# Second layer of a feed-forward block on one Trainium2 core: the rows of the third step move to the first two row places, and the weights of the first product are issued behind the rows of the step ahead

## The chip, the cores and the metric

The kernel runs on one core of a Trainium2 chip. The metric is the time of the slowest core in device microseconds, here of the only one; a kernel's time is the median of its runs. Before the change that is 1913.62 us over three runs, from 1910.7 to 1918.03 us.

## The reference, cut to what matters

One decoder layer over 2048 positions of width 1024: a normed input projection, a pooling mixer and a causal stick-breaking attention, an output projection, then a feed-forward block of inner width 4096 and a last norm. The change lies in the second matrix of the feed-forward block, `w_down`:

```python
        hn2 = rmsnorm(h, norm2_g)
        up = jnp.einsum('bsd,df->bsf', hn2, w_up)
        act = jnp.square(jax.nn.relu(up))
        h = h + jnp.einsum('bsf,fd->bsd', act, w_down)
    return rmsnorm(h, final_g)
```

All of it is float32.

## The kernel before

**Number format.** A float32 operand is split into a high half of the matmul's own type and the rest (`split`: ScalarE copies the high half, line 146, and VectorE subtracts it from the operand, line 147). A product of two float32 tiles is then three matmuls: high by high, high by low, low by high. So no matmul of a step can start before ScalarE's half of the split, and the second one needs VectorE's half too.

**The two layers.** Both feed-forward matrices are multiplied by a seven-product scheme on 2x2 blocks (Strassen's, in Winograd's form). `up` forms the first layer and writes the row sums that the second layer wants to DRAM (`sd`, and `sdi` for the products that are split a second time), all through the SyncE queue SP at lines 884 and 1013. `down` is the second layer. Its products come in the order P1, P6, P7, P4, P5, P2, P3. P1 and P6 have eight steps each, P7 to P2 are split once more into small steps (line 1274), and P3 ends the kernel.

**A step of P1.** `make(g)` prepares step g: it loads one block of weights (`blk`, line 1162, tile `wr`, 512 KB), loads two tiles of rows, one for each pair of token tiles (`ar<-sd`, line 1222, 512 KB each), and splits the weights into `wd` and the rows into two `ad`. The step itself (line 1451) is 48 matmuls, 24 on the first row tile and then 24 on the second. `make_ahead` keeps up to six row tiles and three weight blocks ahead of the matmuls. The first step is made in advance under high priority, the second behind the tile `A22` of the last column of `up`, the rest behind its tile `S3`.

**Places.** Row tiles `ar` lie in two pools: `rs` has two places (`early`), `rs2` three (`late_`). A running number `turns["ar"]` picks the pool in `row`: below 2 it is `rs`, from there on the places are gone through in a ring of five, two of `rs` and three of `rs2`. The number starts at -2, and each step of P1 takes two, so the rows of the first and of the second step lie in `rs`, those of the third in `rs2`. Split rows `ad` have a ring of five as well, split weights `wd` three places (`DA + 1`).

**What sets the order.** Each engine runs its instructions in one fixed order, which a scheduler makes when the kernel is built: it plays through a timeline by rules of its own, and `tc.issue_after(x)` keeps an instruction behind x in it. In P1 the rows of a step are held behind `last[0]`, the row load before them; the weights are not held. All loads and stores named here are issued by SP, in its fixed order. Each of them also waits for one of eight completion counters (`DMAHW0` to `DMAHW7`, used in turn), that is for the transfer eight places ahead of it; a wait named `DVE` is one for VectorE.

Of the kernel before, what the change touches and what calls it, by code (L numbers as in the profile page):

```python
# [46 lines left out]
def hymba_block(ctx: ExitStack, tc: tile.TileContext, xT, gains, w_in, pool_w, w_out, w_up, w_down, out):  # L47
# [95 lines left out]
    def split(dst, src):  # L143

        hi, lo = dst
        nc.scalar.activation(hi, src, AF.Copy)  # L146
        return nc.vector.tensor_tensor(lo, src, hi.bitcast(F32), ALU.subtract)  # L147
# [970 lines left out]
    def down(pools):  # L1118
# [9 lines left out]
            else:  # L1128
                steps += [(n, i, kk, (0, 1)) for kk in range(8)]
        steps += [("P3", S4, kk, (q,)) for q in range(2) for kk in range(8)]  # L1130
        made, turns, extra = {}, {"ar": -2, "ad": 0}, []

        def row(shape, kind, tag, **kw):
            early, late_ = {"ar": rs, "ad": s8}[tag]
            n = turns[tag]
            turns[tag] += 1
            return (early if n < 2 or n % 5 < 2 else late_).tile(shape, kind, tag=tag, name=tag, **kw)
# [11 lines left out]
        def inner_weights(i, kk, t):  # L1149

            if kk < 4:
                tops[i] = t
                return
            b, k = {(x, y): half(w, y) for x, w in enumerate((tops.pop(i), t)) for y in range(2)}, kk - 4
            for to, x, y, p in (((0, 0), (0, 1), (0, 0), "P5"), ((0, 1), (1, 1), (0, 1), "P7"),
                                ((1, 1), (1, 1), (0, 0), "P6"), ((1, 0), (1, 0), (1, 1), "P4")):
                nc.vector.tensor_tensor(b[to], b[x], b[y], ALU.subtract)
                nc.sync.dma_start(wi[i][p][k // 2][:, 2 * (k % 2):2 * (k % 2) + 2], b[to])

        def blk(i, kk, where=None):  # L1160
            t = (where or rt).tile([P, 4, 256], F32, tag="wr", name="wr")
            nc.sync.dma_start(t, w_down[i, kk] if isinstance(i, int) else td[int(i[1]) - 1][kk])
            return t

        def minus(a, b):
            nc.vector.tensor_tensor(b, a, b, ALU.subtract)
            return b

        def more_weights(n, kk, w):

            if n == "P1" and kk % 4 < 2:
                inner_weights(A12, kk, blk(2, kk))
            elif n == "P6":
                minus(blk(2, kk, rtx), w)
                nc.sync.dma_start(half(td[1][kk], 0), half(w, 0))
                if kk >= 4:
                    nc.sync.dma_start(half(td[1][kk], 1), half(w, 1))
                inner_weights(A22, kk, w)

        def make_inner(n, p, kk):  # L1180

            i, kp = SPLIT[n], kk // 2
            if kk % 2 == 0:
                if p in wi[i]:
                    w = rt.tile([P, 4, 256], F32, tag="wr", name="wq")
                    nc.sync.dma_start(w, wi[i][p][kp])
                else:
                    w = quarter(source[n], kp, *{"P1": (0, 0), "P2": (1, 0), "P3": (1, 1)}[p])
                t = made["inner"] = t8.tile([P, 2, 4, 256], F32R, tag="wd", name="wd", align_bytes=256)
            r = row([P, 2, T], F32, "ar")  # L1190
            nc.sync.dma_start(r, {"P1": sd[0][i][kk], "P2": sd[0][i][kk + 4], "P4": sd[1][i][kk + 4]}[p]
                              if p in ("P1", "P2", "P4") else sdi[i][("P5", "P6", "P7", "P3").index(p)][kk])
            if kk % 2 == 0:
                split((t[:, 0], t[:, 1]), w)
            a = row([P, 2, 2, T], F32R, "ad", align_bytes=256)
            split((a[:, 0], a[:, 1]), r)
            return made["inner"], a

        def make(g):
            n, i, kk, qs_ = steps[g]  # L1200
            if qs_ is None:
                at = {("P7", "P5"): 3, ("P5", "P5"): 2}.get((n, i))
                if at is not None and kk == 0:
                    extra[:] = [blk(2, at), blk(2, at + 4)]
                elif at is not None and kk == 3:
                    for k in range(2):
                        inner_weights(A12, at + 4 * k, extra.pop(0))
                made[g] = make_inner(n, i, kk)
                return
            if n != "P3":  # L1210
                kk = TURN[kk]
            b11, b12, b21, b22 = range(4)
            if n == "P1":
                w = blk(b11, kk)
            elif n == "P6":
                w = minus(blk(b22, kk), blk("t1", kk))
            else:
                w = blk(b22, kk)
            rows = {q: row([P, 2, T], F32, "ar") for q in qs_}
            for q in qs_:  # L1220
                with tc.issue_after(last[0].ins) if n == "P1" and last[0] else nullcontext():
                    last[0] = nc.sync.dma_start(rows[q], sd[q][i][kk])
            t = t8.tile([P, 2, 4, 256], F32R, tag="wd", name="wd", align_bytes=256)
            split((t[:, 0], t[:, 1]), w)
            left_ = {}
            for q in qs_:
                left_[q] = row([P, 2, 2, T], F32R, "ad", align_bytes=256)
                last[1] = split((left_[q][:, 0], left_[q][:, 1]), rows[q])
            while late and n != "P1":
                late.pop(0)()  # L1230
            late.append(lambda: more_weights(n, kk, w))
            made[g] = t, left_
# [179 lines left out]
        free, held, ahead, late, last = 4, [], [0, 0, 0], [], [None, None]  # L1412
# [10 lines left out]
        def make_ahead(limit=len(steps)):  # L1423

            while ahead[0] < limit and (ahead[1] + lefts(ahead[0]) <= 6 and ahead[2] + stationary(ahead[0]) <= 3):
                make(ahead[0])
                ahead[1] += lefts(ahead[0])
                ahead[2] += stationary(ahead[0])
                ahead[0] += 1
# [109 lines left out]
    def ffn():  # L1539
        catch_up(len(later))  # L1540
        front_scope.close()
        for _ in layer.pop():
            pass
        left_scope.close()
        with ExitStack() as scope:
            spool = lambda name, bufs, **kw: scope.enter_context(tc.tile_pool(name=name, bufs=bufs, reuse_waits="tile", **kw))

            rlp, pupa = spool("rlp", 2), spool("pupa", 2)
            spool("even", 1).tile([P, 2 * P // 4], F32, name="even")
            rs = spool("rs", 2), spool("rs2", 3)  # L1550
            rt, t8 = spool("rt", 6), spool("t8", DA + 1)
            s8 = spool("s8", 2), spool("s82", 2 * DA - 1)
            tmp2, pup, rtx = spool("tmp2", 2), spool("pup", 6), spool("rtx", 1)
            down([t8, s8, rs, rt, pupa, pup, rtx, rlp, tmp2, spool("psb", 1, space=PS)])
# [88 lines left out]
```

## Time and profile before

| | |
|---|---|
| median of three runs | 1913.62 us |
| the profiled execution's own time | 1912.54 us |
| its span on the core | 1910.7 us |
| TensorE matmul busy | 1882.5 us, 99% |
| VectorE, ScalarE, GpSimd busy | 77%, 54%, 9% |
| data moved | 535.91 MB, 280 GB/s over the span |
| TensorE idle ahead of line 1451 | 7.4 us, once |
| second layer: first matmul of line 1451, last one | 1311.1 us, 1884.0 us |

The profile names a group of instructions by line, engine, operation and tiles, as `pb<-ad,wd`, and puts the idle time of an engine down to what ended it. `PEclk` is the granted TensorE clock as a share of full speed, the DMA share that of the 16 DMA engines that were busy. Times inside the execution are counted from the start of its span.

### The profile page before, as it was taken

How to read it: one execution, taken by the hardware profiler on the slowest of the kernel's cores; microseconds unless marked ns; L12 is line 12 of the kernel's file. 1: busy time of each engine (PE TensorE's matmuls, PEld its weight loads, DVE VectorE, ACT ScalarE, POOL GpSimd, SP SyncE). 2: the span in 40 equal slices, each digit the busy share in tenths (PEclk: the TensorE clock that was granted, in tenths of full speed). 3: DMA queues.
4: the chain of work that ended last, by engine and by line, in shares of the span. 5: the costliest groups of instructions: out<-in, count | busy, mean ns of one | idle time of the engine just before them, and what ended most of it. 6: DMA issues, size and time to landing. Idle time of an engine off the chain costs nothing.

```text
span 1910.7 us, 26756 instructions
## 1 busy us (share of the span) xinstructions
PE 1882.5 (99%) x8947; PEld 1571.0 (82%) x8947; DVE 1480.3 (77%) x2216; ACT 1025.6 (54%) x1616; POOL 180.5 (9%) x399
## 2 busy tenths in 40 slices
PE   9999999999999999999999999998999999999997
PEld 7888888888888888888888888887788888888886
DVE  6887799667866886778789988886556677889774
ACT  6565566555554465554567455554332665656543
POOL 0211123101211030000000000000010010020120
PEclk9999999999999999999999999999999999999999
DMA  7686686888787777887898988889898999999852
GB/s 225 207 271 187 209 283 217 259 303 266 278 328 290 279 245 253 289 311 273 316 342 324 317 302 279 292 294 346 311 314 300 321 318 309 328 303 346 285 209 91
DMA packets 222164, 535.91 MB, mean 280 GB/s; under 512 B 26048, under 2 KB 32192, under 8 KB 218176
## 3 DMA queue, kind: packets, MB, share of 16 engines
q1 hardware_dynamic: 217264, 525.46, 79.4%
q0 software_dynamic: 4608, 8.39, 2.5%
q8 instruction: 72, 1.18, 0.2%
q14 instruction: 76, 0.62, 0.1%
q10 hardware_dynamic: 144, 0.26, 0.0%
HBM read 349.46 MB, written 184.55 MB: 279 GB/s over the span
## 4 chain that ended last, share of the span: by engine, by line
PE 43%; DMA 7%; DVE 5%; issue 1%; ACT 1%; POOL 0%; SPq 0%; DVEq 0%; ACTq 0%
PE pb L1274 16%; PE pb L1451 12%; PE pY L1102 8%; PE pZ L1102 4%; PE pX L1102 2%; DMA t<-in_w_down_dram 2%; DMA sd<-s 1%; DVE hw L147 1%; DMA hn<-hs 1%; PE pb L1391 1%; DMA td<-t 1%; DMA wi_P<-t 1%; DMA sd<-a 1%; DMA ar<-sd 0%; ACT a L1019 0%
## 5 line engine op out<-in xcount | busy, mean ns | idle before, releaser
L1102 PE MATMUL pY<-sa,hw 128*128 128x512 f32 x1536 | 366.2, 389 | 1.6 <-ACT u L1025 1.2
L1102 PEld LDWEIGHTS pY<-sa,hw 128*128 128x128 f32 x1536 | 288.1, 188 | 62.5 <-ACT u L1025 2.0
L1274 PE MATMUL pb<-ad,wd 128*128 128x512 f32 x1344 | 304.8, 389 | 0.0
L178 PE MATMUL pd<-h,hl 128*128 128x512 f32 x752 | 299.7, 399 | 1.0 <-DVE qkr L424 0.7
L180 PE MATMUL pd<-h,hl 128*128 128x512 f32 x752 | 297.0, 395 | 0.0
L179 PE MATMUL pd<-h,hl 128*128 128x512 f32 x752 | 296.9, 395 | 0.0
L1274 PEld LDWEIGHTS pb<-ad,wd 128*128 128x128 f32 x1344 | 252.3, 188 | 52.4
L1451 PE MATMUL pb<-ad,wd 128*128 128x512 f32 x1104 | 255.4, 392 | 7.4 <-ACT ad L146 7.4
L1451 PEld LDWEIGHTS pb<-ad,wd 128*128 128x128 f32 x1104 | 208.2, 189 | 51.0 <-ACT ad L146 7.8
L147 DVE TENSOR_TENSOR ad<-ar,ad 128x1024 fp32r<-128x1024 f32 x160 | 193.9, 1220 | 37.6 <-ACT ad L146 37.0
L146 ACT ACTIVATE ad<-ar 128x1024 fp32r<-128x1024 f32 x160 | 168.3, 1053 | 90.4 <-PE pb L1451 41.1
L1102 PE MATMUL pZ<-sa,hw 128*128 128x512 f32 x768 | 186.6, 389 | 0.9 <-DVE a L1045 0.8
L1102 PEld LDWEIGHTS pZ<-sa,hw 128*128 128x128 f32 x768 | 144.0, 188 | 31.5 <-DVE a L1045 1.2
L178 PEld LDWEIGHTS pd<-h,hl 128*128 128x128 f32 x752 | 142.2, 189 | 28.9 <-DVE qkr L424 1.0
L180 PEld LDWEIGHTS pd<-h,hl 128*128 128x128 f32 x752 | 141.9, 189 | 27.9
L179 PEld LDWEIGHTS pd<-h,hl 128*128 128x128 f32 x752 | 142.0, 189 | 27.0
L146 ACT ACTIVATE hl<-raw 128x512 fp32r<-128x512 f32 x168 | 103.9, 630 | 110.0 <-PE pd L180 66.1
L147 DVE TENSOR_TENSOR hl<-raw,hl 128x512 fp32r<-128x512 f32 x168 | 114.1, 685 | 50.4 <-ACT hl L146 49.7
L1019 ACT ACTIVATE a<-a 128x512 f32<-128x512 f32 x96 | 60.0, 629 | 87.8 <-DVE a L1061 35.9
L147 DVE TENSOR_TENSOR hw<-rt,hw 128x512 fp32r<-128x512 f32 x128 | 86.4, 685 | 23.8 <-ACT hw L146 23.7
L146 ACT ACTIVATE wd<-wq 128x1024 fp32r<-128x1024 f32 x56 | 59.4, 1061 | 80.5 <-PE pb L1274 71.6
L147 DVE TENSOR_TENSOR wd<-wq,wd 128x1024 fp32r<-128x1024 f32 x56 | 68.4, 1222 | 33.7 <-ACT wd L146 32.1
(220 smaller groups left out, 2719.5 us busy)
## 6 DMA issues: line engine op xcount, KB each, us to landing
ar<-sd SPq DMA_DIRECT2D x96, 512.0 KB, 5.6
ar<-sdi SPq DMA_DIRECT2D x64, 512.0 KB, 6.2
rb<-in_w_up_dram SPq DMA_DIRECT2D x30, 1024.0 KB, 6.3
sd<-a SPq DMA_DIRECT2D x104, 256.0 KB, 5.1
raw<-in_w_in_dram SPq DMA_DIRECT2D x50, 512.0 KB, 4.7
sdi<-hr SPq DMA_DIRECT2D x96, 256.0 KB, 5.4
wr<-in_w_down_dram SPq DMA_DIRECT2D x48, 512.0 KB, 5.2
sd<-s SPq DMA_DIRECT2D x88, 256.0 KB, 4.8
```

The costliest lines, as they stand in the source:

```text
L146: nc.scalar.activation(hi, src, AF.Copy)
L147: return nc.vector.tensor_tensor(lo, src, hi.bitcast(F32), ALU.subtract)
L178: nc.tensor.matmul(ps, hl[:, 0, c], hi, start=(k == 0), stop=False)
L179: nc.tensor.matmul(ps, hl[:, 0, c], lo, start=False, stop=False)
L180: mm = nc.tensor.matmul(ps, hl[:, 1, c], hi, start=False, stop=(k == n - 1))
L1019: nc.scalar.activation(t, src, AF.Relu)
L1102: nc.tensor.matmul(t, w[:, wx, c], a[:, ax, c % 2], start=first and c == 0 and x == 0, stop=last and c == G - 1 and x == 2, skip_group_che ...
L1274: nc.tensor.matmul(b, t[:, wx, 2 * (kk % 2) + c, i * P:(i + 1) * P], a[:, ax, c], start=p in ("P1", "P5", "P2") and kk == 0 and c == 0 and ...
L1391: nc.tensor.matmul(b[:, cols], block(t, wx, c, n), a[:, ax, c, cols], start=False, stop=(i == 1 and c == 1 and x == 2), skip_group_check=True)
L1451: nc.tensor.matmul(ps[q, n], block(t, wx, c, n), left_[q][:, ax, c], start=(n_ in ("P1", "P3") and kk == 0 and c == 0 and x == 0), stop=(n ...
```

## The change

Two places in `down`. The running number of row tiles starts at -4, so that three steps of P1, not two, take their rows in the two places of `rs`: the rows of the third step are written over those of the second. And in P1 the load of a step's weights is held behind `last[0]`, the last row load of the step ahead.

```diff
-        made, turns, extra = {}, {"ar": -2, "ad": 0}, []
+        made, turns, extra = {}, {"ar": -4, "ad": 0}, []

         def row(shape, kind, tag, **kw):
             early, late_ = {"ar": rs, "ad": s8}[tag]
...
             if n == "P1":
-                w = blk(b11, kk)
+                with tc.issue_after(last[0].ins) if last[0] else nullcontext():
+                    w = blk(b11, kk)
             elif n == "P6":
```

On SP, this is the stretch from behind the store of `sd_1_4` (the last column of the first layer) to the rows of the third step. `wr` are weights of P1, `sd` and `sdi` the stores of the first layer, `ar<-sd_0_2` the two row tiles of the third step.

```order
-L1162 DMA wr<-in_w_down_dram 128x1024 x2
 L884 DMA sdi_0_0_425<-a_13599 128x512
 L884 DMA sdi_1_0_429<-hr 128x512
-L1162 DMA wr<-in_w_down_dram 128x1024
 L1013 DMA sd_6_4_421<-s_13749 128x512
 L884 DMA sdi_3_0_485<-hr 128x512
 L884 DMA sdi_3_0_437<-hr 128x512
-L1162 DMA wr<-in_w_down_dram 128x1024 x2
-L1222 DMA ar<-sd_0_2_315 128x1024
-L1222 DMA ar<-sd_0_2_371 128x1024
```

Five loads of weights, those of the fourth to the eighth step, leave this stretch; the five stores in it keep their order, and so do the four ahead of it.

The same stretch of SP in the changed kernel, from the first of its rows on, with the waits:

```order
L1223 DMA ar<-sd_0_2_315 128x1024 [waits DMAHW4_49,DVE_49]
L1223 DMA ar<-sd_0_2_371 128x1024 [waits DMAHW5_49,DVE_49]
L1162 DMA wr<-in_w_down_dram 128x1024 [waits DMAHW6_49]
L1223 DMA ar<-sd_0_6_319 128x1024 [waits DMAHW7_49]
L1223 DMA ar<-sd_0_6_375 128x1024 [waits DMAHW0_49]
L1162 DMA wr<-in_w_down_dram 128x1024 [waits DMAHW1_49]
L1223 DMA ar<-sd_0_1_314 128x1024 [waits DMAHW3_49,DMAHW2_49]
L1223 DMA ar<-sd_0_1_370 128x1024 [waits DMAHW4_49,DVE_49]
```

The rows of the third step come behind the stores at once, and now wait for VectorE as well, since the splits of the second step must have read their places; each step's weights then stand between the rows of two steps.

On VectorE, the splits from the second step of P1 on (ScalarE has the same order for its halves):

```order
 L147 TENSOR_TENSOR ad<-ar,ad 128x1024 x2
-L147 TENSOR_TENSOR wd<-wr,wd 128x1024 x3
-L147 TENSOR_TENSOR ad<-ar,ad 128x1024 x6
+L147 TENSOR_TENSOR wd<-wr,wd 128x1024
+L147 TENSOR_TENSOR ad<-ar,ad 128x1024 x2
+L147 TENSOR_TENSOR wd<-wr,wd 128x1024
+L147 TENSOR_TENSOR ad<-ar,ad 128x1024 x2
+L147 TENSOR_TENSOR wd<-wr,wd 128x1024
+L147 TENSOR_TENSOR ad<-ar,ad 128x1024 x2
```

The weights of the third, fourth and fifth step were split one after the other ahead of all rows; now each step's weights are split just ahead of its own rows.

## The prediction

> **What bounds the kernel now.** First the page's busy times, then the waits of TensorE, longest first (waiter, waited-for, us in total, times, longest).
>
> ```profile
> span 1910.7 us, 26756 instructions
> PE 1882.5 (99%) x8947; PEld 1571.0 (82%) x8947; DVE 1480.3 (77%) x2216; ACT 1025.6 (54%) x1616; POOL 180.5 (9%) x399
> PE pb L1451 <- ACT ad L146: 7.4, 1, 7.4
> PE pm L205 <- DVE ss L189: 2.4, 1, 2.4
> ```
>
> TensorE is the bound, so only its holes can be won, and one is larger than all others: a single wait of 7.4 us at line 1451, the first product of the second layer. The timeline of TensorE shows where it lies, that of ScalarE what ended it (start, length, instruction, in brackets the idle time ahead and its releaser):
>
> ```profile
> 1305.55 3.01 PE L1102 MATMUL pY<-sa,hw 128*128 128x512 f32 x12 [0.85 <-ACT u L1025]
> 1311.12 21.92 PE L1451 MATMUL pb<-ad,wd 128*128 128x512 f32 x96
> 1340.44 34.81 PE L1451 MATMUL pb<-ad,wd 128*128 128x512 f32 x143 [7.40 <-ACT ad L146]
> 1324.99 1.06 ACT L146 ACTIVATE wd<-wr 128x1024 fp32r<-128x1024 f32 x1 [0.16 <-DMA wr<-in_w_down_dram]
> 1333.08 1.06 ACT L146 ACTIVATE wd<-wr 128x1024 fp32r<-128x1024 f32 x1 [2.78 <-PE pb L1451]
> 1339.33 1.06 ACT L146 ACTIVATE ad<-ar 128x1024 fp32r<-128x1024 f32 x1 [5.20 <-DMA ar<-sd]
> 1353.76 1.06 ACT L146 ACTIVATE wd<-wr 128x1024 fp32r<-128x1024 f32 x1 [4.38 <-PE pb L1451]
> 1324.86 1.23 DVE L147 TENSOR_TENSOR ad<-ar,ad 128x1024 fp32r<-128x1024 f32 x1 [3.28 <-ACT ad L146]
> 1340.42 6.38 DVE L147 TENSOR_TENSOR ad<-ar,ad 128x1024 fp32r<-128x1024 f32 x5 [5.03 <-ACT ad L146]
> ```
>
> The 96 matmuls are the first two steps. Then ScalarE has the third step's weights split long since (1324.99) but gets its rows only at 1339.33, and TensorE starts 1.11 us later, when the high half is there. The matmul spacing is (21.92 - 0.39) / 95 = 0.2266 us (0.39 is the modelled length of the last one, by the mean of 392 ns in the page's row of that line, the first below; the others are windows):
>
> ```profile
> L1451 PE MATMUL pb<-ad,wd 128*128 128x512 f32 x1104 | 255.4, 392 | 7.4 <-ACT ad L146 7.4
> 1325.00:1332.90 7.90, 7.90 (x36) 6.33 (x34) 3.53 (x3) 2.11 (x2) 0.00 (x0) 1.00 1.04 402
> 1332.90:1340.40 7.50, 0.14 (x1) 0.00 (x0) 1.23 (x1) 2.11 (x2) 0.00 (x0) 0.85 1.03 411
> 1340.40:1345.00 4.60, 4.56 (x11) 3.59 (x12) 4.37 (x4) 3.69 (x4) 0.00 (x0) 0.51 0.88 295
> 1345.00:1350.00 5.00, 5.00 (x24) 4.11 (x23) 2.35 (x3) 1.61 (x2) 0.00 (x0) 1.00 0.95 338
> ```
>
> The rows of windows give, after the busy times of PE, PEld, DVE, ACT and POOL, the granted clock, the DMA share and GB/s. Two things stand in them: the DMA engines are full up to the end of the hole (1.04, 1.03), and the clock is at half (0.51) for 4.60 us after it. So the hole costs twice. The matmul after the 96 could have issued at 1311.12 + 96 x 0.2266 = 1332.87 and issued at 1340.44: 7.57 us. Half clock over 4.60 us: another 2.25 us. Sum 9.8. The two ScalarE rows released by TensorE check it: each splits weights into a place that a finished step frees, at 1333.08 and 1353.76, 20.68 us apart for one step of 48 x 0.2266 = 10.88 us: 9.80 us lost. That is the most that can be won here, 0.51% of 1913.62.
>
> **The change part by part.** Nothing is added to or taken from the work; loads change places. What stands on SP between the third step's weights and its rows is counted by the DMA issues of that stretch (count, KB each, us to landing), and the timeline of SP has their times:
>
> ```profile
> wr<-in_w_down_dram SPq DMA_DIRECT2D x6, 512.0 KB, 7.3
> sdi<-hr SPq DMA_DIRECT2D x5, 256.0 KB, 7.1
> sdi<-a SPq DMA_DIRECT2D x2, 256.0 KB, 7.2
> sd<-a SPq DMA_DIRECT2D x1, 256.0 KB, 6.5
> sd<-s SPq DMA_DIRECT2D x1, 256.0 KB, 7.3
> 1318.39 0.63 SPq L1162 DMA_DIRECT2D wr<-in_w_down_dram  x1
> 1321.67 2.04 SPq L1162 DMA_DIRECT2D wr<-in_w_down_dram  x2
> 1326.12 0.33 SPq L1162 DMA_DIRECT2D wr<-in_w_down_dram  x1
> 1329.17 1.58 SPq L1162 DMA_DIRECT2D wr<-in_w_down_dram  x2
> 1331.07 1.18 SPq L1222 DMA_DIRECT2D ar<-sd  x2
> ```
>
> The first of the six weight loads is the third step's own, the other five are those that the change moves behind the rows. From the landing of that first load (1324.99) to that of the rows (1339.33) come nine stores of 256 KB, five weights and one row tile of 512 KB: 21 units of 256 KB in 14.34 us, 0.683 us each, or 384 GB/s. Ten units go. *Term 1:* the rows land 10 x 0.683 = 6.8 us sooner, at 1332.5; with the fastest of the window rates, 411 GB/s, ten units (2.62 MB) are 6.4 us.
>
> *Term 2, what is left of the hole.* TensorE's first matmul needs the high half, at 1332.5 + 1.1 = 1333.6, that is 0.7 us late. The second needs VectorE's half, which takes 1.23 us more (the row at 1324.86; at 1340.42 it too starts when ScalarE ends), at 1334.8 instead of 1333.1. So 1.7 us stay. The second row tile lands two units, 1.4 us, after the first and is wanted 5.4 us after it (24 matmuls), so it costs nothing. Bounds: by 411 GB/s 2.1 us stay; if the rows came 1.7 us sooner still, nothing.
>
> *Term 3, the clock.* A wait of 0.85 us (the row at 1305.55) did not lower it, the one of 7.40 did. What is left is 0.7 us without any matmul and 1.0 with one, nearer the first: I take the full clock, so 2.25 us are won; the other end is that they stay. The Trainium skill ("TensorE: Matmul & The Clock Gate", Part 1) says that the clock halves after an idle window of about 3.4 us and comes back after a busy one as long. By that a stall of 1.7 us keeps the clock too, and the sum stays; of the two times of the second rival below, which has 2.8 us idle, it gives the shorter. The trace agrees as far as it goes: half clock after 7.40 us idle, full again after 4.6 us of work.
>
> *Term 4, the new waits.* The rows of the third step now wait for VectorE's splits of the second step. The queue reaches them only when the store eight places ahead has landed:
>
> ```profile
> 1319.62 0.38 SPq L884 DMA_DIRECT2D sdi<-a  x1
> ```
>
> That store lands at 1319.62 + 7.2 = 1326.8, the later of the two splits (1324.86) ends at 1326.1, so the wait is over when it is reached: 0 us. Were it later, all of SP would stand behind it. The five weights are now loaded between rows. The fourth step's weights and rows, 1.57 MB or six units, land 4.1 us after the third's, and TensorE has 10.88 us of work by then: 0 us, and the same for each step after it.
>
> *Term 5, what is moved must still be carried,* with TensorE about 8 us ahead of before. Windows of 25 us:
>
> ```profile
> 1350.00:1375.00 25.00, 25.00 (x112) 20.71 (x111) 14.12 (x16) 6.14 (x6) 0.00 (x0) 1.00 0.77 275
> 1375.00:1400.00 25.00, 25.00 (x112) 20.70 (x111) 14.03 (x13) 8.64 (x10) 0.00 (x0) 1.00 0.91 348
> 1400.00:1425.00 25.00, 25.00 (x112) 20.69 (x111) 12.05 (x12) 10.52 (x14) 7.18 (x8) 1.00 0.98 267
> 1414.20 1.42 DVE L1157 TENSOR_TENSOR wr<-wr 128x512 f32<-128x512 f32 x2 [9.12 <-DMA td<-wr]
> 1419.95 1.22 DVE L147 TENSOR_TENSOR ad<-ar,ad 128x1024 fp32r<-128x1024 f32 x1
> 1429.91 1.06 ACT L146 ACTIVATE wd<-wr 128x1024 fp32r<-128x1024 f32 x1 [4.38 <-PE pb L1451]
> 1473.43 1.06 ACT L146 ACTIVATE wd<-wq 128x1024 fp32r<-128x1024 f32 x1 [4.38 <-PE pb L1451]
> 1486.69 1.22 DVE L147 TENSOR_TENSOR ad<-ar,ad 128x1024 fp32r<-128x1024 f32 x1
> ```
>
> Room from 1340.4 to 1400 is 0.12 x 4.6 + 0.05 x 5 + 0.23 x 25 + 0.09 x 25 = 8.8 us of all engines, against 8.1 needed; after that it is 0.98 full. The cushion: ScalarE's split at 1473.43 starts when a step ends, and, with three places, is for use two steps on, at 1473.4 + 21.8 = 1495.2. VectorE's last split for that use ended at 1487.9, 7.3 us ahead. If the transfers after 1400 came no sooner at all, 8.1 - 7.3 = 0.8 us would be lost; if they follow, 0. I take 0.
>
> *Sum.* 9.8 - 1.7 = 8.1 us won, between 7.3 (0.8 lost to term 5) and 9.8, or 5.9 where the half clock stays. From the profiled execution's own 1912.54 us (span 1910.7) that is 1904.4. It lies 1.1 us under the median, so from 1913.62 I predict **1905.5 us**, 0.42% less.
>
> **The rivals.**
> *Hole closed in full.* Rows land before 1330.8 and no half clock: 9.8 us, 1903.8. For it: the last five weights landed no faster than the average, so a stretch without them might run quicker. Against it: it needs 1.7 us more than the bytes give. 17%.
> *Transfers count alike, not by bytes.* Eight are in flight at most, and each landed about 7 us after issue whatever its size (6.5 to 7.3 in the rows above). Then 15 landings in 14.34 us are 0.956 us each, five fewer bring 4.8 us, TensorE's second matmul comes at 1336.9 and 3.8 us stay: 6.0 us won, 1907.6; with the half clock 3.8 won, 1909.8. Against it the share of 1.03 to 1.04: the engines were full with pieces of 256 and 512 KB. The Trainium skill's "DMA: Bandwidth & Descriptors" (Anatomy of one DMA) speaks for it: there a transfer (issued by GpSimd) has a fixed cost of about 2 us beside its bytes, which under some 860 KB is the larger part; this trace, with several in flight, does not show that. 14%.
> *It does nothing:* the rows still wait, now for their places (term 4), because the second step's split slips past the store. It would have to slip by 7 us, with SP standing behind it: 1913.6. 6%.
> *Slower.* One mechanism: VectorE runs in order and stands 9.12 us at 1405 for a store of weights (the row at 1414.20), with the splits of a coming step behind it. If the moved bytes put 6.8 us on such a wait while TensorE is 8.1 us sooner, 14.9 us meet a cushion of about 8.7 (the row at 1419.95 is the last of them, ended at 1421.2; the step that uses them starts as another ends, at 1429.9) and TensorE stalls 6.2, with the half clock 8.4: the gain is gone. It decides from a second wait of that kind on, at 1921. Against it: the room of 8.8 us ahead of it. 6%.
>
> **How the numbers follow.** Forecast 57%, full closing 17%, by count 14%, nothing 6%, slower 6%. Measurements of this kernel tell about 0.5% from no change, 9.6 us, and the three runs of before lie 7.3 us apart. The forecast lies 1.5 us short of that bound and the full closing just past it: faster by over 0.5% gets 0.10 of the 0.17 and about 0.16 of the 0.57, 0.26. Slower by over 0.5%, past 1923, gets 0.04. The rest, 0.70, is within 0.5%. The range, from 1901.0 (full closing less some 2.9 us, the distance of the lowest run from the median) to 1911.0 (by count with the half clock, rounded up), holds the first three cases, of 88% together, less their tails.
>
> **What would show it right or wrong.** Right: the wait of line 1451 on `ad` falls from 7.4 to about 0.7 us; the first `ad` split of the third step starts near 1332.5; the granted clock stays at 1.00 from 1333 to 1350; splits of weights released by TensorE are about 12.6 us apart across the place, not 20.68. Wrong: a new wait of TensorE after 1350, above all between 1400 and 1500, or a hole above 3 us with a half clock behind it.

## The result and the profile after

The changed kernel takes 1904.19 us (median of 12 runs, 1899.78 to 1907.92) against 1912.59 us before (12 runs, 1908.84 to 1918.03). The ratio is 0.9957, with a 95% interval of 0.9946 to 0.9969: 0.43% less, where 0.42% was predicted. The profiled execution took 1904.37 us (span 1902.6 us).

The waits of TensorE in the changed kernel, longest first (waiter, waited-for, us in total, times, longest); line 1452 is the former 1451:

```profile
PE pr L231 <- DVE pc L629: 2.5, 1, 2.5
PE pb L1452 <- ACT ad L146: 1.2, 1, 1.2
```

The wait that was 7.4 us is 1.2 us, and no longer the longest. The timelines of TensorE, ScalarE and VectorE at the place:

```profile
1309.52 21.92 PE L1452 MATMUL pb<-ad,wd 128*128 128x512 f32 x96
1332.69 87.48 PE L1452 MATMUL pb<-ad,wd 128*128 128x512 f32 x383 [1.24 <-ACT ad L146]
1323.37 1.06 ACT L146 ACTIVATE wd<-wr 128x1024 fp32r<-128x1024 f32 x1
1331.58 1.06 ACT L146 ACTIVATE ad<-ar 128x1024 fp32r<-128x1024 f32 x1 [7.15 <-DMA ar<-sd]
1344.28 1.06 ACT L146 ACTIVATE wd<-wr 128x1024 fp32r<-128x1024 f32 x1 [2.60 <-PE pb L1452]
1332.67 2.56 DVE L147 TENSOR_TENSOR ad<-ar,ad 128x1024 fp32r<-128x1024 f32 x2 [6.98 <-ACT ad L146]
```

All times are best read from the first matmul of the second layer, since what lies ahead of it differs from execution to execution: it starts at 1309.52 here and at 1311.12 before, and between 1305.6 and 1314.7 in the profiles below, of changed and unchanged kernels alike. From it the rows' first split comes after 1331.58 - 1309.52 = 22.06 us (before 1339.33 - 1311.12 = 28.21), and the weights' split that the end of the third step releases after 1344.28 - 1309.52 = 34.76 us (before 1353.76 - 1311.12 = 42.64). So 7.88 us are won up to there. Three steps without any loss would take 144 x 0.2266 + 0.21 = 32.84 us (0.21 is the delay from the last matmul's issue slot to that split, 1333.08 - 1332.87 in the profile before): 9.80 us were lost there before, 1.92 us are lost now.

The windows (busy times of PE, PEld, DVE, ACT, POOL, then granted clock, DMA share, GB/s) show what became of the clock and where the moved bytes went:

```profile
1332.90:1340.40 7.50, 7.44 (x32) 5.81 (x32) 7.14 (x7) 6.38 (x6) 0.00 (x0) 1.00 1.03 412
1340.40:1345.00 4.60, 4.60 (x22) 3.78 (x22) 2.44 (x2) 1.79 (x2) 0.00 (x0) 1.00 1.03 411
1350.00:1375.00 25.00, 25.00 (x112) 20.71 (x111) 14.95 (x17) 6.92 (x7) 0.00 (x0) 1.00 0.98 363
```

The clock stays at 1.00 where it was 0.51. The DMA share from 1340.4 to 1345 is 1.03 (0.88 before), from 1350 to 1375 it is 0.98 (0.77 before): the moved weights fill the room that was there.

Not all of the 7.88 us reach the end. Near 1733 us, in the small steps of the second layer, the changed kernel has two waits that the profile before lacks (the timelines, then the window ahead):

```profile
1731.37 1.06 ACT L146 ACTIVATE ad<-ar 128x1024 fp32r<-128x1024 f32 x1 [2.84 <-DMA ar<-sdi]
1733.74 3.01 PE L1275 MATMUL pb<-ad,wd 128*128 128x512 f32 x12 [0.29 <-DVE ad L147]
1737.21 43.14 PE L1275 MATMUL pb<-ad,wd 128*128 128x512 f32 x189 [0.46 <-DVE ad L147]
```

```profile
1700.00:1730.00 30.00, 30.00 (x134) 24.86 (x133) 22.89 (x27) 15.19 (x18) 7.07 (x8) 1.00 1.08 311
```

ScalarE waits 2.84 us for rows there, the window ahead shows the DMA engines full (1.08; the same window is 1.07 in the profile before, so that is nothing new), and TensorE waits for VectorE's half of the split. The last matmul comes 1891.38 - 1309.52 = 581.86 us after the layer's first, against 1899.49 - 1311.12 = 588.37 before: 6.5 us of the gain are in this layer. The other 1.6 us of this one execution lie ahead of the layer, where nothing was changed.

### The profile page after: what moved, and what is told of

The parts are those of the page before. It is cut to its first block, busy times and chain, and to the rows that moved or that the text cites. A ratio compares the mean times of both kernels' runs of the same rounds, so it can differ in the third digit from the quotient of the medians.

```text
span 1902.6 us, 26763 instructions
## 1 busy us (share of the span) xinstructions
PE 1879.0 (99%) x8947; PEld 1568.1 (82%) x8947; DVE 1481.2 (78%) x2216; ACT 1025.2 (54%) x1616; POOL 179.5 (9%) x399
## 3 DMA queue, kind: packets, MB, share of 16 engines
q8 instruction: 72, 1.18, 0.2%
## 4 chain that ended last, share of the span: by engine, by line
PE 49%; DMA 5%; DVE 3%; ACT 1%; issue 1%; POOL 0%; SPq 0%; DVEq 0%; ACTq 0%
PE pb L1275 13%; PE pY L1102 13%; PE pb L1452 12%; PE pZ L1102 7%; PE pX L1102 3%; DMA ar<-sd 2%; DMA ar<-sdi 1%; PE pb L1392 1%; DMA wr<-in_w_down_dram 0%; DMA b<-in_w_down_dram 0%; DMA t<-in_w_down_dram 0%; DMA td<-t 0%; DMA hn<-hs 0%; DVE hw L147 0%; DMA su<-hs 0%
```

## The experiments

One table for all profiles first, each number worked out as above. *Rows* is the time from the layer's first matmul to the first split of the third step's rows; *late* the time by which TensorE's next matmul misses start + 96 x 0.2266; *half* the length of the stretch of half clock at this place, its ends read from windows of 0.5 us; *lost* the loss at the end of the third step; *layer* the time from the layer's first matmul to the last one of the kernel.

| kernel | weight loads ahead of the rows | rows | late | half | lost | layer |
|---|---|---|---|---|---|---|
| before | 5 | 28.21 | 7.57 | 6.83 | 9.80 | 588.4 |
| places only | 5 | 28.20 | 7.56 | 6.83 | 9.84 | 589.1 |
| weights in halves | 5, as 10 halves | 28.70 | 8.06 | 6.83 | 9.64 | 588.6 |
| three ahead | 3 | 25.14 | 4.50 | 6.82 | 7.1 | 586.2 |
| two ahead | 2 | 24.52 | 3.88 | 6.83 | 6.84 | 585.4 |
| one ahead | 1 | 23.13 | 2.49 | 3.41 | 4.00 | 583.2 |
| the change | 0 | 22.06 | 1.42 | 0 | 1.92 | 581.9 |
| the change, second profile | 0 | 23.18 | 2.54 | 3.41 | 4.35 | 583.7 |
| the change, third profile | 0 | 22.11 | 1.47 | 0 | 1.93 | 582.3 |
| weights only | 0 | 22.19 | 1.55 | 0 | 2.05 | 580.9 |
| weights only, second profile | 0 | 22.10 | 1.45 | 0 | 1.93 | 582.0 |
| the change, b22 moved | 0, and no b22 | 16.26 | 0 | 0 | 0 | 579.5 |
| the same, second profile | 0, and no b22 | 16.64 | 0 | 0 | 0 | 579.3 |
| weights only, b22 moved | 0, and no b22 | 19.37 | 0 | 0 | 0 | 579.3 |

(For three ahead the loss is the sum of *late* and half of the 5.31 us that TensorE worked at half clock; the split after the step is released late there for another reason.)

### Which of the two parts does it

The weights' part alone, that is the change with the places as before:

```diff
-        made, turns, extra = {}, {"ar": -4, "ad": 0}, []
+        made, turns, extra = {}, {"ar": -2, "ad": 0}, []
```

> The changed kernel with its second part alone: the weights of the first product are issued behind the rows of the step ahead, while the third step's rows keep the number of turns that they had before. My theory (the ten units of 256 KB that leave the queue ahead of the rows are the whole gain): 0.9957 of the time before, as the changed kernel has, between 0.9945 and 0.997; TensorE's wait on the rows about 1.2 us, no half clock, and some 12.8 us between the two splits of weights that stood 20.68 us apart before. Rival (the earlier place for the rows is what lets them start): 0.999 to 1.001, with the wait at 7.4 us. Rival (both parts have a share): a wait of 3 to 5 us and 0.998.

Measured: 1901.85 us (5 runs, 1900.67 to 1902.6) against 1911.94, ratio 0.9940 (0.9926 to 0.9953). TensorE's wait for the rows is 1.35 us, the clock 1.00.

```profile
1332.00 88.16 PE L1452 MATMUL pb<-ad,wd 128*128 128x512 f32 x386 [1.35 <-ACT ad L146]
```

The two splits lie 10.88 + 2.05 = 12.9 us apart: the loss at this place is that of the changed kernel.

The places' part alone, that is the kernel before with the number of turns at -4:

```diff
-        made, turns, extra = {}, {"ar": -2, "ad": 0}, []
+        made, turns, extra = {}, {"ar": -4, "ad": 0}, []
```

> The kernel before with the first part of the change alone: the third step's rows may lie in the first two places, and so wait for VectorE's splits of the second step, but all five weights stay ahead of them in SP's queue. My theory: nothing moves, 0.999 to 1.001 of the time before, the wait of TensorE 7.4 us (7.0 to 7.8), half clock for 4.6 us behind it; the added wait for VectorE costs 0. Rival (the added wait holds SP): the stores and loads behind it come later, the wait is above 9 us, and the time 1.001 or more. Rival (the place is the gain): 0.997 or less, with a wait of 3 us or less.

Measured: 1911.36 us (10 runs) against 1911.94, ratio 1.0000 (0.9989 to 1.0011), and a wait of 7.38 us:

```profile
1344.03 76.35 PE L1451 MATMUL pb<-ad,wd 128*128 128x512 f32 x326 [7.38 <-ACT ad L146]
1333.15 1.06 ACT L146 ACTIVATE wd<-wr 128x1024 fp32r<-128x1024 f32 x1 [3.50 <-DMA wr<-in_w_down_dram]
1342.92 1.06 ACT L146 ACTIVATE ad<-ar 128x1024 fp32r<-128x1024 f32 x1 [5.18 <-DMA ar<-sd]
```

The rows wait for VectorE's splits there and come no later than before (28.20 us after the layer's start, 28.21 before): the added wait costs nothing, and the places bring nothing. The gain belongs to the weights alone.

The weights' part was timed again with the change itself, because 0.9940 lay below 0.9957 and its profile had no wait near 1733 us:

> The changed kernel, unedited, timed beside the three that follow. Two profiles of it so far: TensorE waits 1.2 us for the third step's rows with the full clock (1.9 us lost there), and 2.4 us with half clock for 3.4 us (4.35 us lost). Theory: its time is 0.9950 to 0.9969 of before, and a third profile has a wait of 1.2 to 2.4 us, with the half clock from some 2 us on. Rival: the first profile is the rule, the second a chance, and its time is that of the kernel with the weights alone, 0.994.

> The weights' part alone, unedited from the earlier run, whose profile lost 2.05 us at the rows and had no stall on VectorE's split near 1733 us. Theory: the two parts together order VectorE's work otherwise after the place, which costs 0.3 to 0.7 us near 1735; so 0.9995 to 0.9998 of the changed kernel's time, too little to tell, and 0.994 to 0.997 of before. Rival: the earlier 0.994 is a real 0.0017 below the changed kernel, and comes again.

Measured: the change 1903.44 us (5 runs), ratio 0.9949 (0.9934 to 0.9963); the weights alone 1904.23 us (6 runs), ratio 0.9954 (0.9938 to 0.9970). The order is now the other way, and the second profile of the weights alone has the waits near 1733 us too:

```profile
1334.47 85.88 PE L1452 MATMUL pb<-ad,wd 128*128 128x512 f32 x376 [1.04 <-ACT ad L146]
1735.64 3.06 PE L1275 MATMUL pb<-ad,wd 128*128 128x512 f32 x12 [0.35 <-DVE ad L147]
1739.11 41.10 PE L1275 MATMUL pb<-ad,wd 128*128 128x512 f32 x180 [0.41 <-DVE ad L147]
```

So the theory that the places cost something there fell; the two kernels can't be told apart. With the second profile of the change,

> The changed kernel once more, unedited, for a second profile. It tells whether the stall of TensorE near 1733 us, 1.4 us that the kernel before does not have, belongs to the change. My theory (the bytes that were moved, with TensorE 8 us ahead, leave VectorE's splits late there): the same two waits at line 1275 on VectorE's split, 0.7 us in all, and a last matmul within 0.5 us of 1891.4. Rival (a chance of one execution): no wait there, and the last matmul 1.4 us sooner, near 1890.0.

which has one wait of 0.46 us there where the same two had been expected, all five profiles of the change and of the weights alone but one show 0.46 to 1.09 us of such waits, and of the three with all five loads ahead one shows 0.34 us. Taking from *layer* what is lost at the rows leaves 578.6, 579.3 and 578.9 us for those three, and 579.9, 579.3, 580.4, 578.9 and 580.1 us for the five: on average 578.9 and 579.7. So about 0.8 us of the gain seem to be given back behind the rows; the five alone lie 1.5 us apart, and the difference is hardly clear of that. That the full DMA engines are the cause is argued from the windows, which were as full before; no run took them away.

### Bytes or landings

The kernel before, with each of the five weight loads made in two:

```diff
-            nc.sync.dma_start(t, w_down[i, kk] if isinstance(i, int) else td[int(i[1]) - 1][kk])
+            src = w_down[i, kk] if isinstance(i, int) else td[int(i[1]) - 1][kk]
+            for x in range(2 if halves else 1):
+                cut = slice(2 * x, 2 * x + 2) if halves else slice(0, 4)
+                nc.sync.dma_start(t[:, cut], src[:, cut])
...
-                w = blk(b11, kk)
+                w = blk(b11, kk, halves=g >= 3)
```

> The kernel before, with each of the five weight loads that stand ahead of the third step's rows made as two loads of 256 KB: the same bytes, ten transfers for five. My theory (the rows wait for bytes): the rows land as before, the wait stays between 7.2 and 8.0 us, time 0.999 to 1.001. Rival (the rows wait for a number of landings, 0.956 us each): five more landings, the wait is 12.2 us, the half clock stays, and the time is 1.0025 of before, 4.8 us more.

Measured: 1912.79 us (10 runs), ratio 1.0005 (0.9994 to 1.0016), and a wait of 7.89 us in place of 7.40:

```profile
1335.40 84.94 PE L1454 MATMUL pb<-ad,wd 128*128 128x512 f32 x367 [7.89 <-ACT ad L146]
```

Five more transfers cost 0.5 us, 0.1 us each, where the rival by count wanted 0.956 us each; and the 0.5 us are no more than what the rows differ by between executions of one kernel (1.1 us in the table). The Trainium skill ("DMA: Bandwidth & Descriptors", Anatomy of one DMA) gives a transfer that GpSimd issues a fixed cost of about 2 us; with several in flight on full engines, issued by SP, this run shows a twentieth of it.

The dose: the change, with the weights held only from a later step on, so that one, two or three of the five loads stay ahead of the rows (4, 5 and 6 in place of the number below):

```diff
-                with tc.issue_after(last[0].ins) if last[0] else nullcontext():
+                with tc.issue_after(last[0].ins) if last[0] and g >= 4 else nullcontext():
```

> The changed kernel, but one of the five weight loads (512 KB) stays ahead of the third step's rows. By bytes (measured in the changed kernel: 8.21 us for 11 units of 256 KB, 0.746 us each): the rows land 1.5 us later than in the changed kernel, TensorE's wait on them is 2.7 us in place of 1.2, the clock stays at 1.00, and the splits of weights on either side lie 14.3 us apart (12.8 in the changed kernel). By count (0.956 us a landing): a wait of 2.2 us, 13.8 us apart. If the clock falls at 2.7 us already, 16 us apart.

> The changed kernel, but two of the five weight loads stay ahead of the third step's rows. By bytes: the rows 3.0 us later than in the changed kernel, a wait of 4.2 us; the clock, by the Trainium skill (TensorE: Matmul & The Clock Gate, Part 1), is halved after some 3.4 us idle. With the half clock for about 4.6 us the splits of weights lie 18.0 us apart, without it 15.8. By count: a wait of 3.1 us and 14.7 us apart, with the full clock.

> The changed kernel, but three of the five weight loads stay ahead of the third step's rows. By bytes: the rows 4.5 us later than in the changed kernel, a wait of 5.7 us, with the half clock behind it (0.5 for 4 to 5 us), and 19.5 us between the splits of weights. By count: a wait of 4.1 us, 17.8 us apart with the half clock, 15.6 without. Both ends of the series are known: none ahead 1.2 us, five ahead (the kernel before) 7.4 us.

Measured, one execution each (1903.67, 1907.17 and 1911.52 us): waits of 2.32, 3.70 and 4.33 us, and 10.88 + 4.00 = 14.9, 17.7 and 18.0 us between the splits (18.9 as the timeline has it, with the late split of the last). From none ahead (22.3 us, the mean of five profiles) to five (28.2, the mean of the first two rows) a load of 512 KB moves the rows by 5.9 / 5 = 1.18 us, and the three between lie on that line within 0.8 us. That is 14% less than the 2 x 0.683 us that the prediction took for it. The expectations by bytes, waits of 2.7, 4.2 and 5.7 us, missed: they took the average of the stretch once more (0.746 us for 256 KB). By the waits alone the first and the last are nearer to the rival by count (2.2 and 4.1 us); it is the halves that speak against the count, not this series. The windows from the third step's weights' split to the rows' show why, first before and then after:

```profile
1324.99:1339.33 14.34, 8.05 (x36) 6.34 (x34) 4.77 (x4) 3.17 (x3) 0.00 (x0) 0.96 1.04 406
```

```profile
1323.37:1331.58 8.21, 8.08 (x36) 6.37 (x34) 2.32 (x2) 1.06 (x1) 0.00 (x0) 1.00 1.05 383
```

Before, 14.34 us at 406 GB/s are 5.82 MB; after, 8.21 us at 383 GB/s are 3.14 MB. The 2.68 MB that are gone had been carried in 6.13 us, at 437 GB/s: faster than the average of what stood there, at the same share of the engines. (Either of the profiles *before* and *places only* against each of the five with no load ahead gives 415 to 453 GB/s by the same working.) What is left, for the most part stores of 256 KB, is slower. Whether that is their size or their direction no run tells.

### The clock

The dose series was to show also how long a wait lowers the clock. One load ahead, and the second profile of the change, each with TensorE's timeline and then windows of 0.5 and 3 us:

```profile
1331.31 88.95 PE L1452 MATMUL pb<-ad,wd 128*128 128x512 f32 x385 [2.32 <-ACT ad L146]
```

```profile
1330.50:1331.00 0.50, 0.00 (x0) 0.00 (x0) 0.00 (x0) 0.50 (x1) 0.00 (x0) 0.95 0.99 401
1331.00:1334.00 3.00, 2.69 (x6) 2.15 (x7) 2.59 (x3) 2.37 (x3) 0.00 (x0) 0.50 1.03 414
1334.00:1334.50 0.50, 0.50 (x3) 0.41 (x2) 0.50 (x1) 0.37 (x1) 0.00 (x0) 0.64 1.02 410
```

```profile
1336.07 84.26 PE L1452 MATMUL pb<-ad,wd 128*128 128x512 f32 x363 [2.36 <-ACT ad L146]
```

```profile
1336.50:1337.00 0.50, 0.50 (x4) 0.33 (x2) 0.50 (x1) 0.50 (x1) 0.00 (x0) 0.73 1.03 418
1337.00:1340.00 3.00, 3.00 (x8) 2.15 (x7) 2.83 (x4) 2.47 (x3) 0.00 (x0) 0.50 1.03 416
1340.00:1340.50 0.50, 0.50 (x3) 0.39 (x2) 0.50 (x1) 0.34 (x1) 0.00 (x0) 0.86 0.98 393
```

A row of 0.5 us whose mean clock is 0.95 has (1 - 0.95) / 0.5 x 0.5 = 0.05 us of half clock in it. So the half clock runs from 1330.95 to 1334.36 in the one and from 1336.73 to 1340.14 in the other: 3.41 us both times, after waits of 2.32 and 2.36 us. In the second profile of the change it begins 0.66 us after TensorE has started again. With two and three loads ahead it lasts 6.83 and 6.82 us, twice as long; with two:

```profile
1334.11 86.10 PE L1452 MATMUL pb<-ad,wd 128*128 128x512 f32 x366 [3.70 <-ACT ad L146]
```

```profile
1333.00:1333.50 0.50, 0.00 (x0) 0.00 (x0) 0.00 (x0) 0.50 (x1) 0.00 (x0) 0.87 1.02 418
1333.50:1340.00 6.50, 5.89 (x14) 4.64 (x15) 5.61 (x5) 5.51 (x6) 0.00 (x0) 0.50 0.94 360
1340.00:1340.50 0.50, 0.50 (x4) 0.38 (x3) 0.50 (x2) 0.00 (x0) 0.00 (x0) 0.80 0.91 352
```

And the kernel with three ahead has it at one more place, behind a wait of 1.79 us in the last step of the first layer:

```profile
1305.34 4.48 PE L1102 MATMUL pY<-sa,hw 128*128 128x512 f32 x12 [1.79 <-ACT u L1025]
```

```profile
1306.50:1307.00 0.50, 0.50 (x3) 0.39 (x2) 0.50 (x1) 0.00 (x0) 0.00 (x0) 0.55 0.68 266
1307.00:1309.50 2.50, 2.50 (x7) 1.96 (x6) 1.14 (x3) 1.26 (x2) 0.00 (x0) 0.50 0.13 52
1309.50:1310.00 0.50, 0.50 (x2) 0.35 (x2) 0.16 (x1) 0.14 (x1) 0.00 (x0) 0.54 0.00 0
```

That is 1306.55 to 1309.96, 3.41 us again; twelve matmuls that take 3.01 us elsewhere took 4.48. Behind its wait for the rows the half clock of the same profile begins at 1337.50 - 0.23 = 1337.27:

```profile
1337.00:1337.50 0.50, 0.00 (x0) 0.00 (x0) 0.00 (x0) 0.00 (x0) 0.00 (x0) 0.77 0.96 393
```

The two starts are 30.72 us apart, nine times 3.413. That is so everywhere: in each of the fourteen profiles all changes of the clock lie whole multiples of 3.413 us apart, and where this grid lies differs from execution to execution. So the clock changes only at the ends of windows of that length, which run on whatever the kernel does, and a wait is cut up by them. What counts, by these profiles, is TensorE's idle time within one window. With only the places changed, the half clock begins at 1342.00 - 0.16 = 1341.84:

```profile
1341.50:1342.00 0.50, 0.00 (x0) 0.00 (x0) 0.00 (x0) 0.00 (x0) 0.00 (x0) 0.84 1.06 434
```

The window ahead of that start, from 1338.43, is idle throughout; the one before it, in which the wait begins at 1344.03 - 7.38 = 1336.65, holds 1.79 us of idle time and left the clock alone. With three ahead a window with 1.79 us was followed by half clock. Among the windows between the wide matmuls of lines 1102 and 1451 (1452), at full clock, 1.24 to 1.64 us idle lowered it in none, 1.79 us in one of two, and 1.96 us and more in all: 1331.31 - 2.32 = 1328.99 to 1330.95, that is 1.96 us, with one ahead, 2.36 us in the second profile of the change. The line lies at about half of a window (52%) there.

Near 450 us, between narrow matmuls, less is enough. In the third profile of the change 0.69 us did it:

```profile
445.14 1.02 PE L205 MATMUL pm<-inv,ss 128*128 128x1 f32 x8 [0.69 <-DVE ss L189]
```

```profile
446.50:449.50 3.00, 3.00 (x12) 2.52 (x11) 0.87 (x2) 0.28 (x1) 0.00 (x0) 0.50 0.99 266
```

That matmuls of one column count for less than their busy time is a guess from this place; no run tests it. At line 231, near 460 us, a wait of 1.58 us lay whole within one window in the first profile of the version below, and the clock fell; with one and with two loads ahead the grid cut the same wait, with 1.21 and 1.35 us in the larger part, and it did not.

The Trainium skill ("TensorE: Matmul & The Clock Gate", Part 1) counts in windows of 3413 ns that run freely, and puts the half clock behind an idle window. The grid agrees with the length and with the free running. But the window need not be idle throughout: here about half of it was enough.

So the change stands near that edge. Its wait is 1.24 us in the first profile and 1.30 us in the third, but 2.36 us, all within one window, in the second. There it lost 2.54 us idle and 3.41 / 2 = 1.7 us by the clock, 4.35 in all where the first and the third lost 1.9, and took 1908.52 us. Why its rows landed 1.1 us later than in the other two stays open.

### A version with the rest of the hole closed

In the changed kernel one more load of weights, `b22` of the pre-additions, still stands ahead of the rows, and waits on SP for TensorE. Moved behind a row load as well:

```diff
             elif n == "P6":
-                minus(blk(2, kk, rtx), w)
+                with tc.issue_after(last[0].ins):
+                    b22 = blk(2, kk, rtx)
+                minus(b22, w)
```

> The changed kernel, and beside it the load of the weight block b22 that is subtracted is issued behind the step ahead of it too. In the changed kernel that load stands in SP's queue ahead of the third step's rows and waits there for TensorE's last matmul of the first layer, with the DMA engines idle for some 2 us near 1307. My theory (what is left of the hole, 1.9 us, is that wait of SP): the rows land 2 us sooner, TensorE's wait falls from 1.2 to 0, up to 1.9 us are won: 0.9947 to 0.9957 of the time before, 0.999 to 1.000 of the changed kernel. Rival (the wait on TensorE goes with the load that takes the same place, and the later b22 holds VectorE's subtraction): no gain or a loss, 0.9957 to 0.998 of before.

> The changed kernel with the load of b22 moved behind its step as well, unedited from the earlier run, whose profile has no wait for the third step's rows at all (0 us lost there). Theory: 1.9 to 4.4 us below the changed kernel of this call, 0.9977 to 0.9990 of it, and 0.9935 to 0.9955 of before. Rival (earlier 0.995 is what it has): what is won there is lost ahead of the layer, and its time is within 1 us of the changed kernel's.

> The weights' part alone and the load of b22 moved as well: the two that were best each by its own part. Theory: no wait for the third step's rows (0 us), no stall on VectorE's split near 1733 us, last matmul 578.9 to 579.5 us after the second layer's first (589 before, 581.9 and 583.7 in two profiles of the changed kernel): 0.9930 to 0.9950 of before. Rival: with the places as before the rows cannot start early enough and the wait is 1 us or more again.

Measured: 1902.09 us (5 runs), ratio 0.9950 (0.9937 to 0.9964), and again 1901.55 us (6 runs), ratio 0.9937 (0.9921 to 0.9952); with the weights' part alone 1901.17 us (5 runs), ratio 0.9942 (0.9927 to 0.9957). In all three profiles TensorE runs through the place without a wait, as in the second of them:

```profile
1309.53 115.76 PE L1454 MATMUL pb<-ad,wd 128*128 128x512 f32 x510
```

Nothing is lost at the rows, and the layer is 579.3 to 579.5 us long, 2.8 us less than the average of the five profiles of the change and of the weights alone (582.2), and shorter than each of them (580.9 at the least). Against the kernel before, the version takes 0.5 to 0.6% less. That it also beats the change is shown by the length of the layer; the whole times only lean that way. Timed side by side, its 11 runs have a mean of 1901.27 us and the five of the change 1902.49, a difference of 1.2 us with an interval of -1.1 to 3.6, which leaves room for none. Over all runs, timed on different occasions, it is 2.5 us (16 runs against 18, 0.8 to 4.3). The reason given for the version was wrong in part. SP's wait for TensorE (2.1 us at line 1162 in the changed kernel) is gone, but the idle stretch of the DMA engines that was to go with it is not:

```profile
SPq L1162 <- PE pY L1102: 2.1, 1, 2.1
```

```profile
1306.00:1307.00 1.00, 1.00 (x6) 0.84 (x5) 0.44 (x1) 0.53 (x1) 0.00 (x0) 1.00 0.01 2
1307.00:1308.00 1.00, 1.00 (x6) 0.81 (x5) 0.85 (x2) 0.96 (x2) 0.00 (x0) 1.00 0.00 0
```

```profile
SPq L1013 <- ACT a L1020: 4.0, 2, 2.1
```

```profile
1306.00:1307.00 1.00, 1.00 (x6) 0.84 (x5) 0.06 (x1) 0.87 (x2) 0.00 (x0) 1.00 0.01 2
1307.00:1308.00 1.00, 1.00 (x6) 0.81 (x5) 1.00 (x2) 0.96 (x2) 0.00 (x0) 1.00 0.22 88
```

The first is the changed kernel, the second the version in its second profile: SP stands 4.0 us for ScalarE there (2.3 us in the changed kernel), and the DMA share is nearly as low. Over the 9 us from 7 us ahead of the layer's first matmul the engines idle 3.8 to 4.0 us in the three profiles of the version, and 3.7 to 4.3 us in the five of the change and of the weights alone. With the weights alone the rows come 22.1 - 19.4 = 2.7 us sooner. One load of 512 KB less ahead of them is 1.2 us of that by the dose series; what the other 1.5 us are was not taken apart. With both parts the edit does one thing more: the scheduler puts the first row load of the third step ahead of the last five stores of the first layer (issued at 1319.93 in the second profile, the other row load at 1325.28), and so the first rows come at 16.3 and 16.6 us. Where `b22` is loaded instead, it costs nothing that the length of the layer shows.

## Why the prediction was right, point by point

**Bound and hole.** TensorE's one large hole was what could be won, 9.80 us, and the time fell by 8.0 us (1912.27 to 1904.29, the means of all 53 and 18 runs).

**Term 1** was mis-sized. The rows came 6.15 us sooner, not 6.8 (5.0 to 6.1 in the other four profiles without loads ahead). The step that failed is "ten units at 0.683 us each": an average over weights and stores was used for weights alone, which were carried at 437 GB/s. The other end that the term named, 6.4 us by 411 GB/s, was nearer. That it is bytes that count stands by the halves: 0.5 us for five more transfers.

**Term 2** came out in size, 1.92 us where 1.7 were worked out, but by two errors that cancel, and that is luck. The first matmul is 1.42 us late (0.7 predicted: the rows landed later than term 1 had it), and the wait for VectorE's half is 0.5 us (1.0 predicted). The second is an error of mechanism: the prediction, and the account of the kernel ahead of it, have the second matmul of a step wait for VectorE's half. TensorE's weight loads (`PEld`, one ahead of each matmul) show that in the changed kernel four matmuls go first and the fifth waits:

```profile
1332.69 0.76 PEld L1452 LDWEIGHTS pb<-ad,wd 128*128 128x128 f32 x4 [1.67 <-ACT ad L146]
1333.95 0.53 PEld L1452 LDWEIGHTS pb<-ad,wd 128*128 128x128 f32 x3 [0.50 <-DVE ad L147]
```

In the code the second matmul does use that half, but the order that runs is the scheduler's. The first four cover 4 x 0.2266 = 0.9 us of the 1.23 us that VectorE's half takes. The second row tile cost nothing, as VectorE's half of it ends at 1332.67 + 2.56 = 1335.2 and the step's second half comes at 1332.69 + 24 x 0.2266 = 1338.1.

**Term 3** was right in the profiled execution, with a clock of 1.00 from 1332.9 to 1345, and in four of the five profiles without loads ahead. But its margin was far smaller than it held: a stall of 1.7 us was taken to be safe, and a window with 1.79 us idle lowered the clock in one profile of two, while the rows come up to 1.1 us later in one execution than in another. In the second profile of the change the wait was 2.36 us, and half clock for 3.41 us cost it another 1.7.

**Term 4** was right: the places alone, with their wait for VectorE, leave the hole at 7.38 us and the ratio at 1.0000.

**Term 5** took 0 of its 0 to 0.8 us, and about 0.8 seem to have gone. It looked for the place between 1400 and 1500, where VectorE's waits for stores are long, and nothing happened there; the waits came near 1733, behind a window of 1.08 of the DMA engines (1.07 before), which the prediction does not treat. The room behind the hole took the moved bytes as worked out.

**The sum.** 8.1 us were predicted for the profiled execution, and 1904.37 us came where 1904.4 stood. Of that match some is chance: 7.88 us were won at the place, 1.4 given back by the end of the layer (588.37 - 581.86 = 6.5 stay), and 1.6 came from ahead of the layer, which varies by itself.

**The rivals.** The hole did not close in full (1.92 us stay); it takes one more load moved. Transfers do not count alike (the halves). The rows do not wait for their places instead (the two kernels with one part each). The slower case did not come: no wait of TensorE between 1350 and 1500; VectorE's longest wait for a transfer is 5.15 us there, where the profile before had 9.12.

## What to carry to other kernels

On a full in-order queue, what stands ahead of an urgent load and is wanted later costs its own bytes, at its own rate, and holding it back is worth just that; a place in memory that comes free earlier is worth nothing while the queue ahead is what is late. A hole of TensorE between wide matmuls should be brought well under half of a clock window, 1.7 us, and not only under 3: up to 1.64 us idle in a window the clock stayed, from 1.96 us on it fell, and the same kernel showed a wait of 1.24 us in one execution and of 2.36 in another. When a hole is won, look for new waits anywhere behind it, not only near by: here the next ones came 400 us later.

## What was not expected of the hardware

The half clock began and ended only on a grid of 3.413 us, which lies differently in each execution. So it came in stretches of one or two windows, 3.41 or 6.83 us, whatever the wait's own length, and once began 0.66 us after TensorE had already started again. About half of a window idle was enough to lower the clock, and to bring it back more work was needed: with two loads ahead a second slow window followed although the first held 1334.11 - 1333.37 = 0.74 us of idle time only, while with one load ahead 1331.31 - 1330.95 = 0.36 us of idle time let the clock come back after one. By the difference of two windows, weights of 512 KB went at 437 GB/s where the whole stretch, with stores of 256 KB, averaged 406.
